# A list scheduler's cost table: one issue time for matmuls and transposes over the whole kernel

## The chip, the cores and the metric

The kernel runs on one core of a Trainium2 chip. The metric is the device time of one execution in microseconds; each kernel is run several times, and the median counts. One further execution is recorded by the profiler. The names of the profile are used throughout: PE is TensorE's matmuls, PEld its weight loads, DVE is VectorE, ACT is ScalarE, POOL is GpSimd, SP is the engine whose queue issues the weight transfers.

## The reference, cut to what matters

One layer of a bidirectional hybrid encoder with 512 tokens and 1024 channels in float32. Two branches mix tokens side by side, are gated and merged, and a SwiGLU feed-forward follows.

```python
h = rmsnorm(x, mix_norm[l])
p = h @ w_in[l]
rx, ry, qkv, z, ba, gates = jnp.split(p, SPLIT_IDX, axis=-1)
y_rnn = rglru_branch(rx, ry, ...) @ w_rnn_proj[l]
y_dn = deltanet_branch(qkv, z, ba, ...) @ w_dn_proj[l]
g_rnn, g_dn = jnp.split(jax.nn.sigmoid(gates), 2, axis=-1)
x = x + (g_rnn * y_rnn + g_dn * y_dn) @ w_out[l]
h = rmsnorm(x, ffn_norm[l])
gt, up = jnp.split(h @ w_gate_up[l], 2, axis=-1)
x = x + (jax.nn.silu(gt) * up) @ w_down[l]
...
return rmsnorm(x, final_norm)
```

The recurrent branch (RG-LRU) works on 1536 channels in 12 blocks of 128: a short convolution, two sigmoid gates per direction, an exponential, a square root, and a linear scan forwards and backwards. The DeltaNet branch has 8 heads of 128: convolutions and SiLU for q, k and v, norms, a triangular solve for each chunk of tokens, and a state that is carried from chunk to chunk, in both directions.

## The kernel before, in words

**Tiling.** Channels lie on the 128 partitions and the 512 tokens along the free axis. A weight matrix is streamed in pieces of 128 x 1024 floats (768 or 256 for the branch projections). Each piece is loaded into `wraw` by SP's queue, rounded to fp32r by ScalarE (`whi`), and the remainder is formed by VectorE (`wlo`). The activations are split the same way into `hh` and `hl`. A projection of one output block is then three sets of matmuls into one PSUM bank: `whi` with the high and with the low activations, and `wlo` with the high ones. With 8 contraction steps that is 24 matmuls of 512 columns. `whi` and `wlo` have two buffers each, `wraw` three.

**Stages.** The norm and its transposes come first (some 23 us). Then the recurrent blocks run in four groups of three (`rg_front`, `rg_mid`, `rg_out`); a group's sigmoids, its tanh and exponentials, its square roots and the GELU of its second projection need different tables on ScalarE, and each change of table is an `ACT_TABLE_LOAD`. Then the DeltaNet heads go through in four pairs (`dn_front`, `dn_mats`, `dn_inverse`, `dn_state`, `dn_out`), interleaved with the gate projections (`rnn_gate`, `dn_gate`). In `dn_inverse` a chain of some sixty small VectorE instructions inverts 32 x 32 blocks by substitution and ends in two stream transposes, after which TensorE joins the blocks. `dn_state` is a chain between TensorE, which fills a PSUM bank, and ScalarE or VectorE, which copies or combines it for the next step. At the end of the branch `dn_part(0, 6, n)` projects the first six heads and `dn_part(6, 2, n)` the last two, whose tiles come out of the last `dn_out`. The output projection, the feed-forward (gate/up products by a seven-product scheme) and the down projection follow.

**Order.** No instruction is issued where it is written. Every call on an engine goes through the class `Rec`, which books a cost in ns for it and appends it to `Plan.ops` with its dependences on tiles. At the end `Plan.order` runs a list schedule over all of them: it keeps a time for each engine, and lets an engine that is free in that plan take the ready instruction with the smallest due time whose buffers can be had. The due times come from the place in the source (`plan.t`, advanced by `spend`) and from a list of 156 numbers, `TIMES`, which give the base time of each stage in units of 100 ns. For ScalarE an instruction that needs another table than the loaded one is put back by `SWITCH` (12,000 ns) in that comparison, but taken when nothing else is ready. The engines then run the found sequence in program order, with semaphores for the dependences, so that a cost in the table changes nothing but the sequence.

**The table for TensorE.** `Rec` books a matmul by its columns n, lines 351 to 356:

```python
if op == "transpose" and self.plan.fixed > 3:
    cost = 110
elif four_:
    cost = 33 if cols == 32 else 81 if cols == 64 else n * 4 / 2.4
else:
    cost = max(n / 2.4, 107 if rhs.dtype == F32R else 54) + (self.plan.fixed if rhs.dtype == F32R else 2.5)
```

`four_` is true for plain float32 operands. `Plan.__init__` sets `fixed` to 2.5 (line 78), and the body of the kernel sets it to 13.3 at line 1209, behind the first half of the output projection. ScalarE and VectorE costs are booked 10% longer than their formulas (`SLACK`), and results pass between engines after fixed delays (`LAG`).

Of the kernel before, what the change touches and what calls it, by code (L numbers as in the profile page):

```python
# [54 lines left out]
class Plan:  # L55
# [10 lines left out]
    def __init__(self, nc):  # L66
        self.nc = nc
        self.ops = []
        self.where, self.bases = [], []
        self.t = self.base = 0.0  # L70
        self.stage = 0
        self.tags = {}
        self.tile_tag = {}
        self.hist = {}
        self.keep = set()
        self.extra = ()
        self.admit = ()
        self.fixed = 2.5

    def tile(self, pool, shape, dt, tag, bufs, name):  # L80
        ap = pool.tile(list(shape), dt, tag=tag, name=name, bufs=bufs)
# [298 lines left out]
def trunk(ctx: ExitStack, tc: tile.TileContext, x, mix_norm, w_in, rg_conv_w, rg_conv_b, rg_wa, rg_ba, rg_wx, rg_bx,  # L380
# [3 lines left out]
    plan = Plan(nc)  # L384
# [34 lines left out]
    def four(dt=F32, shape=(P, 2, 512)):  # L419
        return new(t4, shape, "t4", N4, dt)  # L420
# [747 lines left out]
    def weights_w(src):  # L1168
        now = plan.t
        raw = new(wp, (P, 2, 512), "wraw", 3)  # L1170
        hi = four(F32R)
        lo = four(F32R)
        plan.t = now - 20
        Q.dma_start(raw, src)
        plan.t = now - AHEAD
        A.copy(hi, raw)
        V.tensor_tensor(lo, raw, f(hi), ALU.subtract)
        plan.t = now
        return hi, lo
# [12 lines left out]
    def wo_part(k2, half):  # L1192
        return wo[:, 2 * k2:2 * k2 + 2, half * 512:(half + 1) * 512]
# [12 lines left out]
        V.tensor_scalar(sb, sa, 1.0 / D, EPS, ALU.mult, ALU.add)  # L1206
        ssh.append(sb)
    ws = [weights_w(wo_part(k2, 1)) for k2 in range(4)]
    plan.fixed = 13.3
    a1 = [four(shape=(P, 4, 256)) for _ in range(2)]  # L1210
    a2 = [four(shape=(P, 4, 256)) for _ in range(2)]
    for c in range(NT):
# [240 lines left out]
```

## Time and profile before

| | us |
|---|---|
| median of 3 runs | 1095.43 |
| their range | 1092.89 to 1096.24 |
| the profiled execution | 1094.72 |
| its span in the profile | 1093.0 |

| engine | busy, us | instructions |
|---|---|---|
| PE | 1069.0 | 6916 |
| DVE | 828.9 | 1489 |
| ACT | 625.3 | 1125 |
| POOL | 44.2 | 93 |

The profiled execution is one of its own, and its time and span differ by 1.7 us that lie outside the recorded instructions. All instructions carry line 374, the line of the recording helper, so that places are told by tile and time: `mm`, `ax` and `st` are the three kinds of PSUM bank, `t` is any of the shared work tiles. In a timeline a row is start, length, engine, line, operation, result and operands, the number of instructions merged, and in brackets the idle time before them with what ended it. A row's time may overlap the next row's, since instructions of one engine overlap in flight; the distance between two starts is the time that the engine spends on one.

### The profile page before, as it was taken

The numbers are of one execution on the slowest core, as the hardware profiler recorded it, in microseconds if no ns is written. First come the engines' busy times: TensorE is split into PE (matmuls) and PEld (weight loads), VectorE is DVE, ScalarE is ACT, GpSimd is POOL, SyncE is SP. The second block draws the span as 40 slices with busy tenths as digits, with TensorE's granted clock in tenths as the row PEclk, the third lists the DMA queues.
The fourth block names the chain that finished last, engine by engine and source line by source line (L and its number), as shares of the span: only waits on it lengthen the run. The fifth ranks groups of instructions, "written<-read, shape, count | busy, mean of one in ns | idle before, by whom it ended". The sixth has DMA issues, their size and how long they took to land.

```text
span 1093.0 us, 17606 instructions
## 1 busy us (share of the span) xinstructions
PE 1069.0 (98%) x6916; PEld 933.9 (85%) x6916; DVE 828.9 (76%) x1489; ACT 625.3 (57%) x1125; POOL 44.2 (4%) x93
## 2 busy tenths in 40 slices
PE   7999999999999999999999999999999999999997
PEld 6988788887888887888798887789999999988886
DVE  6777999779895898599749847768988988872432
ACT  6868987887348644765575254446544454451223
POOL 2000000002020100020010000000000000000000
PEclk9999999999999999999999999999999999999999
DMA  7333323232321133104302313442233333333222
GB/s 194 96 107 86 97 63 87 82 92 76 102 78 55 49 102 97 40 20 119 93 18 58 93 54 111 134 127 67 81 114 114 99 99 117 103 110 97 97 97 77
DMA packets 160787, 98.40 MB, mean 90 GB/s; under 512 B 4800, under 2 KB 151344, under 8 KB 160704
## 3 DMA queue, kind: packets, MB, share of 16 engines
q1 hardware_dynamic: 159232, 93.99, 29.5%
q10 hardware_dynamic: 1184, 3.15, 0.8%
q8 instruction: 54, 0.88, 0.3%
q0 software_dynamic: 288, 0.13, 0.1%
q14 instruction: 29, 0.24, 0.1%
HBM read 95.17 MB, written 2.10 MB: 89 GB/s over the span
## 4 chain that ended last, share of the span: by engine, by line
PE 83%; DVE 3%; ACT 2%; issue 0%; DVEq 0%; ACTq 0%
PE mm L374 48%; PE ax L374 20%; PE st L374 15%; DVE t L374 3%; ACT na L374 1%; ACT t L374 1%; DVE wlo L374 0%; ACT ax L374 0%; ACT whi L374 0%; ACT L374 0%; DVE na L374 0%; DVEq L1448 0%; ACT drt L374 0%; ACT rst L374 0%; DVE nq L374 0%
## 5 line engine op out<-in xcount | busy, mean ns | idle before, releaser
L374 ACT CAST whi<-wraw 128x1024 fp32r<-128x1024 f32 (+2 forms) x150 | 146.4, 977 | 220.2 <-PE mm L374 109.9
L374 DVE TENSOR_TENSOR wlo<-wraw,whi 128x1024 fp32r<-128x1024 f32 (+2 forms) x149 | 169.2, 1137 | 129.4 <-ACT whi L374 94.4
L374 PE MATMUL mm<-hh,whi 128*128 128x512 f32 (+2 forms) x704 | 242.0, 356 | 1.1 <-ACT whi L374 1.1
L374 PE MATMUL mm<-hl,whi 128*128 128x512 f32 (+2 forms) x704 | 241.6, 355 | 0.0
L374 DVE TENSOR_TENSOR t<-t,t 128x512 fp32r<-128x512 f32 (+17 forms) x414 | 213.2, 525 | 15.7 <-ACT t L374 8.6
L374 PE MATMUL mm<-hh,wlo 128*128 128x512 f32 (+1 forms) x688 | 153.9, 355 | 1.1 <-DVE wlo L374 1.1
L374 PEld LDWEIGHTS mm<-hh,whi 128*128 128x128 f32 (+1 forms) x704 | 132.4, 188 | 18.7 <-ACT whi L374 1.9
L374 PEld LDWEIGHTS mm<-hl,whi 128*128 128x128 f32 (+1 forms) x704 | 132.4, 188 | 17.1 <-DVE hl L374 0.2
L374 PEld LDWEIGHTS mm<-hh,wlo 128*128 128x128 f32 x688 | 116.0, 189 | 18.6 <-DVE wlo L374 1.5
L374 PE MATMUL ax<-t,t 32*32 32x32 f32 (+3 forms) x876 | 89.8, 262 | 0.8 <-issue 0.7
L374 PE MATMUL mm<-t,whi 128*128 128x512 f32 x320 | 82.0, 398 | 2.6 <-ACT t L374 1.8
L374 DVE SCALAR_TENSOR_TENSOR t<-mm,par,t 128x511 f32<-128x511 f32 (+1 forms) x108 | 80.0, 744 | 3.7 <-ACT t L374 2.9
L374 PEld LDWEIGHTS ax<-t,t 128*128 128x128 f32 (+1 forms) x876 | 74.7, 153 | 8.2 <-ACT t L374 1.6
L374 ACT ACT_TABLE_LOAD x58 | 74.4, 1283 | 5.8 <-PEq L1439 1.7
L374 ACT CAST t<-t 128x512 fp32r<-128x512 f32 (+1 forms) x95 | 64.5, 685 | 22.7 <-DVE t L374 21.0
L374 PEld LDWEIGHTS mm<-t,whi 128*128 128x128 f32 x320 | 59.9, 190 | 17.4 <-ACT t L374 2.4
L374 PE MATMUL mm<-t,t 128*128 128x256 f32 (+1 forms) x372 | 66.4, 322 | 0.0
L374 ACT ACTIVATE t<-t 128x128 f32<-128x128 f32 (+4 forms) x84 | 45.8, 558 | 23.8 <-DVE t L374 20.3
L374 PEld LDWEIGHTS mm<-t,t 128*128 128x128 f32 x372 | 54.7, 191 | 5.2 <-ACT t L374 0.3
L374 PE MATMUL mm<-t,wlo 128*128 128x512 f32 x160 | 43.0, 396 | 0.0
L374 PE MATMUL st<-hh,whi 128*128 128x512 f32 (+1 forms) x112 | 42.0, 378 | 0.0
L374 PE MATMUL st<-hl,whi 128*128 128x512 f32 (+1 forms) x112 | 41.8, 378 | 0.0
(219 smaller groups left out, 1804.9 us busy)
## 6 DMA issues: line engine op xcount, KB each, us to landing
wraw<-in_w_in_dram SPq DMA_DIRECT2D x72, 512.0 KB, 3.8
wraw<-in_w_gate_up_dram SPq DMA_DIRECT2D x44, 512.0 KB, 3.9
wraw<-in_w_down_dram SPq DMA_DIRECT2D x22, 512.0 KB, 3.7
wraw<-in_w_rnn_proj_dram SPq DMA_DIRECT2D x16, 384.0 KB, 3.6
wraw<-in_w_out_dram SPq DMA_DIRECT2D x8, 512.0 KB, 4.5
wraw<-in_w_dn_proj_dram SPq DMA_DIRECT2D x8, 384.0 KB, 3.6
t<-in_x_dram SPq DMA_DIRECT2D x4, 512.0 KB, 5.1
na<-in_x_dram ACTq DMA_DIRECT2D x4, 512.0 KB, 6.1
```

The costliest lines, as they stand in the source:

```text
L374: self.plan.add(e, lambda: real(*a, **kw), outs, ins, cost, tail, table)
```

## The change

The start value of `fixed` becomes 13.3, and the line that set it later is dropped. So all fp32r matmuls ahead of that line are booked 10.8 ns longer, and all transposes ahead of it (plain float32, 128 columns of result) at 110 ns in place of 512/2.4 = 213 ns. `TIMES`, `SLACK`, `LAG`, the dependences and the instructions stay as they are; the list schedule is run again with the new table.

```diff
         self.keep = set()
         self.extra = ()
         self.admit = ()
-        self.fixed = 2.5
+        self.fixed = 13.3
...
     ws = [weights_w(wo_part(k2, 1)) for k2 in range(4)]
-    plan.fixed = 13.3
     a1 = [four(shape=(P, 4, 256)) for _ in range(2)]
```

## The prediction

> **What bounds the kernel now.** I read the page first, then busy time by stage, then the timelines of the places where TensorE waits.
>
> ```profile
> span 1093.0 us, 17606 instructions
> PE 1069.0 (98%) x6916; PEld 933.9 (85%) x6916; DVE 828.9 (76%) x1489; ACT 625.3 (57%) x1125; POOL 44.2 (4%) x93
> 30.00:690.00 660.00, 649.47 (x4071) 543.93 (x4071) 528.52 (x984) 427.14 (x784) 37.58 (x72) 1.00 0.27 78
> 690.00:1093.00 403.00, 396.75 (x2709) 369.64 (x2707) 282.34 (x461) 178.58 (x303) 0.00 (x0) 1.00 0.33 102
> 60.00:93.00 33.00, 26.10 (x40) 1.00 0.34 96
> 93.00:145.00 52.00, 45.24 (x59) 1.00 0.29 82
> ```
>
> The third and fourth lines are stages: from, to, length, then busy time of PE, PEld, DVE, ACT and POOL. The last two give ACT alone. TensorE is the bound nearly everywhere. No instruction's work changes, so only its idle time can. From 30 to 690 us, where the two orders differ most, that is 660 - 649.5 = 10.5 us, plus a slow clock and small gaps between overlapping records. More than some 12 us can't be won; the loss has no such limit. Around 93 to 145 us ScalarE is nearly full too, with 52 - 45.24 = 6.76 us idle.
>
> **What the edit changes in the table.** It moves the 13.3 to the start. Until line 1209 a 512-column fp32r matmul was booked at 512/2.4 + 2.5 = 215.8 ns; now it is 226.6. A 128-column transpose falls from 213 to 110.
>
> ```profile
> 275.83 1.98 PE L374 MATMUL mm<-hh,wlo 128*128 128x512 f32 x8
> 277.65 0.39 PE L374 MATMUL mm<-hh,whi 128*128 128x512 f32 x1
> na<-in_x_dram ACTq DMA_DIRECT2D x4, 512.0 KB, 6.1
> ```
>
> Eight matmuls take 277.65 - 275.83 = 1.82 us, 227 ns each, so the new entry is the true one here. The program issues the same matmuls, casts and transfers; the two built orders differ in sequence, and ScalarE carries 60 table loads in place of 58. The last 571 rows of TensorE's order are the same. The weight queue on SP shifts only in its first 50 rows, mostly gate loads against main weights. None of TensorE's waits below is on a transfer, so I cost that at nothing; what hides it is that a landed tile waits for its cast, and if this cover went, the cast would start late by what the transfer lacks. The four transfers on ScalarE's queue (last line above, 6.1 us to land) move ahead of one 0.84 us cast near 667 us; their tile is first used after 690 us, behind the first half of the output projection, and that hides them.
>
> **Part A, the recurrent-gate stage: ScalarE's queue.**
>
> ```profile
> 104.12 1.28 ACT L374 ACT_TABLE_LOAD   x1
> 105.41 1.09 ACT L374 ACTIVATE t<-st 128x512 f32<-128x512 f32 x2
> 110.21 0.78 ACT L374 ACTIVATE t<-mm,zero_t,par 128x512 f32<-128x512 f32 x1 [3.70 <-PE mm L374]
> 110.89 1.98 ACT L374 CAST whi<-wraw 128x1024 fp32r<-128x1024 f32 x2
> 112.77 1.34 ACT L374 ACTIVATE t<-t,rgt 128x512 f32<-128x512 f32 x2
> 116.05 0.60 ACT L374 CAST t<-t 128x512 fp32r<-128x512 f32 x1
> 119.43 1.32 ACT L374 ACTIVATE t<-t,rgs 128x512 f32<-128x512 f32 x2
> L374 ACT CAST t<-graw 128x512 fp32r<-128x512 f32 x12 | 7.4, 616 | 1.1 <-DMA graw<-in_rg_wx_dram 1.1
> 111.97 0.50 PE L374 MATMUL mm<-hh,whi 128*128 128x512 f32 x1 [1.11 <-ACT whi L374]
> 115.73 0.39 PE L374 MATMUL mm<-hh,whi 128*128 128x512 f32 x1
> 120.63 2.12 PE L374 MATMUL mm<-hh,wlo 128*128 128x512 f32 x8 [1.12 <-DVE wlo L374]
> ```
>
> Before the cast at 110.89 the new order has four more table loads, 4 x 1.28 = 5.1 us, because it fits exponentials between the sigmoids of two blocks. It also issues those blocks' gate matmuls 4 to 5 us later on TensorE, so ScalarE would have stood idle there, and 3.70 us idle stand at 110.21. I take the loads as absorbed up to this cast. The row at 110.89 is two casts back to back. In the new order the second follows a gate cast (0.6, pipelined 0.55), two tanh (1.34), a load (1.28), two exponentials (1.32) and a cast (0.55): 5.0 us more, so it ends near 111.9 + 5.0 + 1.05 = 118.0. TensorE wants it at 115.73, at an unchanged place: 2.3 us late. The wait at 120.63 (start 1.3 us late) goes in exchange: VectorE's order there hardly changes, and its tile is ready when TensorE gets there. Net **+1.1 us**. Late next would be the cast at 120.66 for the block after, but there the new order gives TensorE more to do first.
>
> ```profile
> 144.28 1.05 ACT L374 CAST whi<-wraw 128x1024 fp32r<-128x1024 f32 x1
> 148.63 3.78 ACT L374 ACTIVATE t<-t,rgt 128x512 f32<-128x512 f32 x6
> 152.31 0.61 ACT L374 CAST t<-t 128x512 fp32r<-128x512 f32 x1
> 151.60 0.39 PE L374 MATMUL st<-hh,whi 128*128 128x512 f32 x1
> ```
>
> The cast at 144.28 is put behind the six tanh, another load (1.28) and an exponential (0.7): 152.3 + 2.0 + 1.05 less the 0.95 that it vacated, 154.4, against a use at 151.60 (0.2 later in the new order). That is 2.6 late; TensorE is already 1.1 behind, which leaves **+1.5**. Bounds for A: nothing, if ScalarE gives back its idle time ahead of the cast (33 - 26.10 = 6.9 and 6.76 us, against 15.3 us more work summed with the old durations); 15.3 less the old margin of 6.5 = 8.8, if none. I take +2.6, nearest to the walk along the rows.
>
> In sentences that the sum can do without: the Trainium skill, page "ScalarE: Activation LUTs", section "What ACT_TABLE_LOAD costs", charges each switch with about 1283 ns and a drain of about 1380 ns. The trace agrees with the load, but not here with the drain: 104.12 + 1.28 = 105.40, and the next activation starts at 105.41. By that page four loads would cost another estimated 5.5 us and the sum would be near 1102.
>
> **Part B, the ends of the DeltaNet substitutions.** Four times a VectorE chain of some 30 us hands its result to TensorE.
>
> ```profile
> 324.41 4.17 DVE L374 STREAM_TRANSPOSE t<-t 128x1024 f32<-128x1024 f32 x2
> 329.07 0.75 PE L374 MATMUL ax<-t,na 32*32 32x32 f32 x64
> 437.05 0.74 PE L374 MATMUL ax<-t,na 32*32 32x32 f32 x64 [1.09 <-DVE t L374]
> 534.72 0.47 PE L374 MATMUL ax<-t,na 32*32 32x32 f32 x33 [0.41 <-DVE t L374]
> 630.60 0.74 PE L374 MATMUL ax<-t,na 32*32 32x32 f32 x64 [0.75 <-DVE t L374]
> ```
>
> In the new order TensorE has 1.59, 1.36 and 4.53 us less work ahead of the first, third and fourth of these places, and 0.45 more ahead of the second (matmuls counted at 227 ns); VectorE has 0.96 less ahead of the fourth, and the same ahead of the others. The first had 329.07 - 328.58 = 0.49 us to spare: +1.1. The second gives 0.45 back, the third loses 1.36. At the fourth the chain no longer stands behind the low-part cast that follows it, and it can use idle time of VectorE: 0, though 3.4 if it can't. Sum **+2.0**; bounds 0 (idle time absorbs all) and +5.4.
>
> **Part C, the covers of the state chain.** After each short group TensorE fills the time until ScalarE's copy.
>
> ```profile
> 642.96 1.05 PE L374 MATMUL st<-t,na 128*128 128x128 f32 x8
> 643.77 0.94 PE L374 MATMUL mm<-t,wlo 128*128 128x512 f32 x3
> 645.23 1.05 PE L374 MATMUL st<-t,t 128*128 128x128 f32 x8
> 644.05 0.59 ACT L374 COPY t<-st 128x512 f32<-128x512 f32 x1 [0.21 <-PE st L374]
> ```
>
> From 643.77 to 645.23, 1.46 us of fill cover a copy that ends at 644.64. Of 59 such steps 31 had six matmuls (1.36 us) or more; in the new order 27 have, and 29 have about five (1.13 us) against 24. A free ScalarE needs about 0.9 us, so most stay covered; a copy behind a 1.05 us cast does not. I take **+0.4**, bounds -1 and +2.
>
> **Part D, the last two heads' transposes.**
>
> ```profile
> 676.66 1.03 PE L374 MATMUL ax<-ident,t 128*128 128x128 f32 x8
> 678.05 1.40 DVE L374 SCALAR_TENSOR_TENSOR t<-ax,par,t 128x512 f32<-128x512 f32 x2
> 678.83 1.28 ACT L374 CAST t<-t 128x512 fp32r<-128x512 f32 x2 [2.29 <-DVE t L374]
> 679.50 0.50 PE L374 MATMUL mm<-t,whi 128*128 128x512 f32 x1 [1.81 <-ACT t L374]
> 680.71 1.11 PE L374 MATMUL mm<-t,whi 128*128 128x512 f32 x3 [0.70 <-DVE t L374]
> 681.30:685.50 4.20, 4.20 (x12) 2.83 (x12) 2.41 (x5) 1.33 (x3) 0.00 (x0) 0.60 0.11 31
> ```
>
> Here TensorE has nothing to fill in: 1.81 + 0.70 us idle, and then a granted clock of 0.60 (the last line's third number from its end), in which twelve matmuls take 4.20 in place of 12 x 0.227 = 2.72 us. Together 4.0. The new order puts these transposes 7.5 us earlier and ten matmuls of the previous projection behind them (2.3 us), then the rest in between. The low part still comes about 0.6 us late and VectorE's normalised tile perhaps 0.4. I take **-3.0**, bounds -4.2 and -1. Beside this: the Trainium skill, page "TensorE: Matmul & The Clock Gate", section "What's actually happening", halves the clock after an idle window of about 3.4 us. The trace agrees with the half clock, but not with the length: the two waits here, 2.5 us in all, were enough. By the page the clock's 1.5 us would not be there to win, and the sum would be near 1098.
>
> **Sum.** 2.6 + 2.0 + 0.4 - 3.0 = +2.0 us. The profiled execution took 1094.72 us, 1.7 beside its span; that makes **1096.7 us**. That execution lies 0.7 under the median of the runs shown, 1095.43, so the forecast is 0.1% over the median.
>
> **Rivals.** *ScalarE becomes the bound of the gate stage* (slower): its idle time there stays a wait for TensorE, as at 110.21, and all 8.8 us of A reach the casts: 1094.7 + 8.8 + 2.0 + 0.4 - 3.0 = **1102.9**. For it: 87% busy. Against: the later gate matmuls leave room. It decides once over half of the 13.7 us idle can't be given back. *A truer table packs better* (faster): A and B are absorbed, C gives 1 and D 4.2: **1089.5**. For it: 227 ns, and the idle rows of B and D; against it: the unchanged priorities, under which the casts above move back. *The edit changes nothing that counts*: the stalls only trade places, **1094.7**; for it TensorE's equal work, against it the concrete rows of D.
>
> **How the numbers follow.** The forecast has 0.39 (its own range 1093 to 1100), ScalarE's queue 0.29, better packing 0.21, nothing 0.11. The bounds sum to 1094.7 + 0 + 0 - 1 - 4.2 = 1089.5 and 1094.7 + 8.8 + 5.4 + 2 - 1 = 1109.9; both ends together are unlikely, so the range is **1089 to 1107**. About 0.3% (3.3 us) is what a measurement of this kernel can tell from no change. Over 1098.7 lie the second case and a third of the first: 0.43. Under 1092.1 lies the third and a little of the first: 0.23. The rest, 0.34, is within.
>
> **What would show it.** Right: a wait of TensorE for the cast near 116 and one near 154 us; the waits of 1.81 and 0.70 us near 680 and the clock of 0.60 gone; waits for VectorE of 1 to 2 us at the four substitution ends; 60 table loads. Wrong: ScalarE waiting for TensorE at 110 for less than a microsecond while TensorE waits for it (then A is larger), or TensorE idle for some 4 us at the fourth substitution end, where B has 0.

## The result, and the profile after

The changed kernel takes 1097.75 us (median of 11 runs, 1096.56 to 1101.12) against 1094.81 for the kernel before beside it. The ratio of the means is 1.0032 (of these medians 1.0027), 95% interval 1.0022 to 1.0042. It is slower, by about the 0.3% that a measurement of this kernel can tell. The profiled execution took 1096.93 us, 2.2 more than that of before.

The head of the page, then the table of stretches (from, to, length, busy time of PE, PEld, DVE, ACT and POOL, granted clock, DMA share, GB/s):

```profile
span 1095.2 us, 17616 instructions
PE 1070.3 (98%) x6916; PEld 933.7 (85%) x6916; DVE 826.6 (75%) x1489; ACT 626.6 (57%) x1127; POOL 46.1 (4%) x93
```

```profile
30.00:690.00 660.00, 648.65 (x4060) 541.55 (x4059) 524.01 (x979) 425.59 (x782) 39.46 (x72) 1.00 0.27 77
...
93.00:145.00 52.00, 48.36 (x203) 38.75 (x202) 46.46 (x52) 46.29 (x61) 1.43 (x3) 0.97 0.25 70
118.00:123.50 5.50, 5.28 (x16) 4.27 (x17) 5.50 (x8) 4.88 (x9) 0.00 (x0) 0.69 0.07 15
```

Work and counts are the same but for ScalarE's two more table loads; the other eight new instructions are semaphore operations. TensorE has lost time, and the third and the fourth line show one place: a clock of 0.69, with VectorE busy for all of the 5.50 us.

To see where the 2.2 us lie I took, for each matmul of both traces, its start less the usual distances (227 ns for 512 columns, 120 for 256, 112 for a transpose, 52 and 15 for the small tiles) of everything ahead of it on TensorE. What remains is time lost up to there, and the difference of the two kernels at the same amount of work done says where one lost more:

| stretch, in us of TensorE's work | after less before, us | the forecast's term |
|---|---|---|
| up to 100 (113 us of the trace) | -0.2 | 0 |
| 100 to 200 (113 to 214 us of the trace): the gate stage | +4.8 | A: +2.6 |
| 200 to 300 | -1.3 | 0 |
| 300 to 640: the DeltaNet heads | +3.3 | B and C: +2.4 |
| 640 (668 us of the trace) to the end: the last two heads' transposes | -4.4 | D: -3.0 |
| sum | +2.2 | +2.0 |

The places in the timeline of the changed kernel (start, length, engine, operation; idle time ahead in brackets). TensorE in the gate stage:

```profile
115.31 0.39 PE L374 MATMUL mm<-hl,whi 128*128 128x512 f32 x1
118.22 0.79 PE L374 MATMUL mm<-hh,whi 128*128 128x512 f32 x1 [2.52 <-ACT whi L374]
118.81 0.63 PE L374 MATMUL mm<-hl,whi 128*128 128x512 f32 x1
119.24 0.63 PE L374 MATMUL mm<-hh,whi 128*128 128x512 f32 x1
```

ScalarE, whose cast at 117.13 is the one waited for:

```profile
102.31 2.01 ACT L374 ACTIVATE t<-t 128x1024 f32<-128x1024 f32 x2
...
110.65 1.03 ACT L374 CAST whi<-wraw 128x1024 fp32r<-128x1024 f32 x1
...
114.76 1.34 ACT L374 ACTIVATE t<-t,rgs 128x512 f32<-128x512 f32 x2
116.60 0.62 ACT L374 CAST t<-t 128x512 fp32r<-128x512 f32 x1 [0.50 <-DVE t L374]
117.13 1.04 ACT L374 CAST whi<-wraw 128x1024 fp32r<-128x1024 f32 x1
```

The square roots at 102.31 began in the kernel before at

```profile
101.14 2.96 ACT L374 ACTIVATE t<-t 128x1024 f32<-128x1024 f32 x3
```

TensorE stood still for 118.22 - 115.31 - 0.23 = 2.68 us and then ran at half speed: the next eight matmuls took 121.71 - 118.22 = 3.49 us (121.71 is the start of the ninth) in place of 8 x 0.227 = 1.82, six of them 0.43 us from one to the next. That is another 1.7 us. The cast stands behind two exponentials and a small cast that itself waited for VectorE, whose chain began 1.17 us later with the square roots. TensorE at the ends of the four substitutions and at the last transposes:

```profile
331.44 0.75 PE L374 MATMUL ax<-t,na 32*32 32x32 f32 x64 [0.57 <-DVE t L374]
...
443.14 0.74 PE L374 MATMUL ax<-t,na 32*32 32x32 f32 x64 [0.42 <-DVE t L374]
...
539.09 0.75 PE L374 MATMUL ax<-t,na 32*32 32x32 f32 x64 [0.81 <-DVE t L374]
...
631.64 0.74 PE L374 MATMUL ax<-t,na 32*32 32x32 f32 x64 [0.83 <-DVE t L374]
...
675.77 0.60 PE L374 MATMUL ax<-ident,t 128*128 128x128 f32 x4
676.12 0.48 PE L374 MATMUL mm<-t,whi 128*128 128x512 f32 x1
676.44 0.60 PE L374 MATMUL ax<-ident,t 128*128 128x128 f32 x4
676.79 2.10 PE L374 MATMUL mm<-t,whi 128*128 128x512 f32 x8
...
687.11 0.73 PE L374 MATMUL mm<-t,wlo 128*128 128x512 f32 x2 [0.51 <-DVE wlo L374]
```

All four ends wait now, each for less than a microsecond. Behind the transposes TensorE goes straight on with earlier matmuls; of the 4 us that stood there, 0.5 of waiting is left.

### The profile page after: what moved, and what is told of

It is laid out like the page before. It is cut to its first block, busy times and chain, and to the rows that moved or that the text cites. A ratio compares the mean times of both kernels' runs of the same rounds, so it can differ in the third digit from the quotient of the medians.

```text
span 1095.2 us, 17616 instructions
## 1 busy us (share of the span) xinstructions
PE 1070.3 (98%) x6916; PEld 933.7 (85%) x6916; DVE 826.6 (75%) x1489; ACT 626.6 (57%) x1127; POOL 46.1 (4%) x93
## 4 chain that ended last, share of the span: by engine, by line
PE 87%; DVE 7%; ACT 4%; issue 1%; DMA 1%; SPq 0%; DVEq 0%
PE mm L374 50%; PE ax L374 22%; PE st L374 15%; DVE t L374 5%; ACT t L374 2%; DVE wlo L374 1%; ACT na L374 1%; DMA wraw<-in_w_in_dram 1%; DVE na L374 1%; ACT whi L374 1%; ACT L374 0%; DVE hl L374 0%; ACT ax L374 0%; SPq L374 0%; ACT hh L374 0%
## 5 line engine op out<-in xcount | busy, mean ns | idle before, releaser
L374 DVE TENSOR_TENSOR t<-t,t 128x512 fp32r<-128x512 f32 (+16 forms) x414 | 212.4, 524 | 17.0 <-ACT t L374 10.4
```

The lines of the kernel that those rows point to most:

```text
L374: self.plan.add(e, lambda: real(*a, **kw), outs, ins, cost, tail, table)
```

## Experiments

All runs in one table. "Loss" is the measure above against the trace of before, by stretch of TensorE's work; the medians stand beside 1093.9 to 1094.8 us for the kernel before in the same runs. The stretch up to 100, -1.4 to +0.8, is left out.

| run | median, us | ratio (95%) | 100-200 | 200-300 | 300-640 | 640-end |
|---|---|---|---|---|---|---|
| the change | 1097.75 | 1.0032 (1.0022-1.0042) | +4.8 | -1.3 | +3.3 | -4.4 |
| matmuls only | 1104.90 | 1.0104 (1.0091-1.0118) | +4.9 | -0.1 | +8.7 | -2.9 |
| transposes only | 1124.73 | 1.0279 (1.0265-1.0293) | 0.0 | -0.5 | +26.0 | +4.6 |
| from the DeltaNet heads on | 1102.24 | 1.0071 (1.0058-1.0084) | 0.0 | -1.2 | +6.9 | -0.1 |
| last pair of heads only | 1093.24 | 0.9991 (0.9982-0.9999) | 0.0 | 0.0 | 0.0 | -1.3 |
| 12.3 for 13.3 | 1108.84 | 1.0133 (1.0118-1.0148) | +15.6 | -1.6 | +3.2 | -3.5 |
| before, cast back | 1099.29 | 1.0047 (1.0035-1.0060) | +4.5 | 0.0 | -0.6 | +0.8 |
| after, cast forward | 1099.60 | 1.0049 (1.0035-1.0062) | +5.7 | -1.2 | +4.0 | -4.1 |
| after, four moved | 1100.22 | 1.0059 (1.0046-1.0073) | +6.0 | -1.2 | +3.1 | -3.8 |
| before, three moved | 1093.05 | 0.9993 (0.9984-1.0002) | -0.7 | 0.0 | -0.6 | -0.3 |
| after, exponentials together | 1099.97 | 1.0049 (1.0033-1.0066) | +7.2 | -1.3 | +3.0 | -3.6 |
| searched, from after | 1114.03 | 1.0186 (1.0172-1.0200) | +6.6 | +0.1 | +16.7 | -4.8 |
| searched, from last pair only | 1111.73 | 1.0158 (1.0144-1.0172) | +7.5 | +0.8 | +14.2 | -3.7 |

Where rows run one and the same sequence (the changed kernel and its three edits, or the kernel before and its two, all behind 200) they differ by up to 1.1 us in a stretch. A difference of a microsecond between two rows is therefore not told from none.

### What the late cast costs

In the kernel before, the cast is put seven ScalarE operations later in the found sequence (with `moved`, the operations that need it); no other engine's order changes.

```diff
         todo = plan.order()
+        acts = [i for i in todo if plan.ops[i][0] == "ACT"]
+        end = todo.index(acts[acts.index(cast) + 7]) + 1
...
+        todo = [i for i in todo[:end] if i not in moved] + moved + todo[end:]
```

> The kernel before with one instruction elsewhere: the same cast stands seven ScalarE operations later (two tanh, a table load, two exponentials, a tanh and two small casts come first), so that it ends near 118.5 us against a use at 115.73. Theory of the late cast: a wait of 2.8 us, some 1.6 us of half clock behind it, less the 1.3 us wait for the low part at 120.63 that goes: +3.1 us, about 1097.9; +1.8, about 1096.6, if the wait of 1.31 us at 249 gives that much back. Theory that the half clock belongs to something else in the changed order: +1.5 or less, no granted clock under 0.9 near 120.

TensorE's timeline, and the stretch behind it:

```profile
115.31 0.39 PE L374 MATMUL mm<-hl,whi 128*128 128x512 f32 x1
119.70 0.50 PE L374 MATMUL mm<-hh,whi 128*128 128x512 f32 x1 [4.00 <-ACT whi L374]
```

```profile
119.00:124.00 5.00, 4.30 (x12) 3.39 (x13) 3.79 (x5) 4.06 (x6) 0.00 (x0) 0.66 0.42 111
```

One cast, late by 4.2 us, costs 4.5 us that nothing behind it gives back: 4.2 of waiting, some 1.7 of slow clock, less the 1.3 us wait for the low part that goes. (The expected 3.1 was for a wait of 2.8.) The wait at 249 us stayed as it was, so its going in the changed kernel belongs to the new sequence there.

A late cast thus brings a wait and half clock, as in the change. It does not explain the whole of the change's +4.8, because the wait is shorter there: 2.68 of waiting and 1.7 of slow clock, less 1.4 for the low part (the 1.28 and a slow matmul behind it), make 3.0 us at that place. The other 1.8 lie in four smaller stalls of 0.4 to 0.6 us near 141, 155, 181 and 200 us, which no run moved alone.

### Whether moving the cast takes it away

```diff
         todo = plan.order()
+        todo.remove(cast[1])
+        todo.insert(todo.index(cast[0]) + 1, cast[1])
```

> The changed kernel with one instruction elsewhere: ScalarE's cast that TensorE waits 2.68 us for at 118.22 stands directly behind the cast before it, five operations earlier. Theory of the late cast: the wait of 2.68 us and the slow clock behind it (1.7 us) go, the wait of 1.3 us for the low part near 120 comes back, and the time falls by about 3.1 us to some 1094.7. Theory that ScalarE's whole work bounds the stage: the operations that the cast passes come 1.05 us later, TensorE waits for one of them instead, and the time stays at 1097 to 1098.

It doesn't. (In the sequence the cast passes six operations and a table load; the text above says five.) TensorE, and VectorE's row for what it then waits for, in this run and in the kernel before:

```profile
118.67 0.39 PE L374 MATMUL mm<-hl,whi 128*128 128x512 f32 x1
122.47 2.58 PE L374 MATMUL mm<-hh,wlo 128*128 128x512 f32 x8 [3.41 <-DVE wlo L374]
124.85 0.63 PE L374 MATMUL mm<-hh,whi 128*128 128x512 f32 x1
```

```profile
121.20 2.36 DVE L374 TENSOR_TENSOR wlo<-wraw,whi 128x1024 fp32r<-128x1024 f32 x2
```

```profile
119.36 1.22 DVE L374 TENSOR_TENSOR wlo<-wraw,whi 128x1024 fp32r<-128x1024 f32 x1
```

The first of the two low parts ends some 1.2 us after 121.20, and TensorE starts at 122.47. Behind the late cast stood an equally late low part, covered only because TensorE was already waiting. The 3.6 us from 118.67 + 0.23 to 122.47 add up: 1.28 were waited there in the kernel before, the low part starts 1.84 us later, and TensorE is through with the matmuls ahead of it 0.46 us earlier (118.90 for 119.13 + 0.23), having four fewer of them.

So the next edit, with a helper that puts one operation ahead of another in the found sequence, moves four operations: the late cast (756); both low parts (865 and 757), ahead of two scans and three small operations; and the next cast (980) by five operations, ahead of a small cast that waits for VectorE:

```diff
+        put(756, 1592)
+        put(865, 443)
+        put(757, 443)
+        put(980, 729)
```

> The changed kernel with four instructions elsewhere near 110 to 125 us: the late cast directly behind the one before it, the next cast four operations earlier, and two low parts on VectorE ahead of the two scans that they stood behind. The run before had the late cast moved alone, and TensorE waited 3.58 us for a low part in its place. Theory of two chains equally late (cast on ScalarE, low part on VectorE): with both moved neither wait remains, the 2.68 us and the 1.7 us of slow clock go, and the time falls by some 4.3 us to 1093.4. Theory that the whole stage is bound by ScalarE's or VectorE's work: TensorE waits 2 to 4 us for a third thing before 160 us, and the time is 1096 to 1098.

```profile
128.49 0.44 PE L374 MATMUL mm<-hh,whi 128*128 128x512 f32 x1
132.59 1.22 PE L374 MATMUL ax<-t,t 128*128 128x512 f32 x2 [3.66 <-ACT t L374]
```

Both waits are gone, and 3.9 us appear ten microseconds later, at the gate matmuls of a block whose split activations come through VectorE and ScalarE. VectorE is full here, so the low parts moved forward push its two scans back, from 116.48 to 119.04 us, and what hangs on the scans is late instead. The theory of two late chains falls; that of a stage bound by the work behind the square roots fits, though the expected 1096 to 1098 was too low. The last three of these moves in the kernel before:

> The kernel before with the same two low parts and the same next cast moved forward. Theory of two chains: the wait of 1.28 us at 120.63 goes and nothing takes its place, 1093.1 us against 1094.4. Theory that the stage is bound by the work: the wait of 1.3 us reappears before 160 us, and the time stays at 1094.4.

There the wait of 1.3 us becomes one of 0.6 near 132, a gain of 0.7 us that the timing (0.9993, 0.9984 to 1.0002) doesn't tell from none. So neither kernel gains by these moves.

### Whether the table loads are the cause

Two exponentials that stand alone between two table loads each are put with the next ones.

```diff
         todo = plan.order()
+        for i in (418, 419):
+            todo.remove(i)
+            todo.insert(todo.index(422), i)
```

> The changed kernel with two exponentials of the first block, which each stand alone between two table loads near 82 and 90 us, put right ahead of the next exponential at 97.5: 56 table loads in place of 60, 4 x 1.28 = 5.1 us less work on ScalarE ahead of the square roots. Theory that the loads were absorbed by ScalarE's idle time (the prediction's step): the square roots at 102.31 don't come earlier, since they wait for what TensorE delivers, the wait of 2.7 us at 118 stays, and the time stays within 1 us of the changed kernel's 1097.7. Theory that the loads fill ScalarE's queue up: the square roots and with them VectorE's low parts come 2 to 4 us earlier and the time falls by 2 to 4 us.

ScalarE's groups and its timeline:

```profile
L374 ACT ACT_TABLE_LOAD x56 | 71.8, 1283 | 5.7 <-PEq L1441 1.7 <-PE ax L374 1.5 <-PE mm L374 0.8
```

```profile
85.89 0.69 ACT L374 ACTIVATE t<-ax,par 128x512 f32<-128x512 f32 x1 [2.69 <-PE ax L374]
...
94.05 0.69 ACT L374 ACTIVATE t<-ax,par 128x512 f32<-128x512 f32 x1 [2.24 <-PE ax L374]
...
103.70 2.01 ACT L374 ACTIVATE t<-t 128x1024 f32<-128x1024 f32 x2
```

Four loads fewer, and ScalarE idles instead, waiting for TensorE's gate matmuls: the loads were absorbed, as the prediction had it. But the two exponentials now stand in the part that isn't idle, the square roots begin 1.4 us later, TensorE's wait for the cast grows from 2.68 to 3.95 us, and the time from 1097.75 to 1099.97, which neither theory had. The square roots' start passes on nearly one for one (1.39 us there, 1.27 at the wait): from there to the cast runs a chain through a full VectorE. In the change that chain starts 1.17 us late, and not because of these four loads; that it is the gate matmuls, which the new sequence issues later, is what these idle times suggest, but no run moved them alone.

### Whether the change is the sum of its parts

The matmuls' entry alone, and the transposes' entry alone, each from the start:

```diff
+        self.turns = False
...
-                if op == "transpose" and self.plan.fixed > 3:
+                if op == "transpose" and self.plan.turns:
...
+    plan.turns = True
```

> One part of the change alone: the matmuls at 226.6 ns from the start, the transposes still at 213 ns up to line 1209. Theory of places: the gate stage has hardly a transpose, so its loss of 3.5 to 4.8 us comes back in full, the DeltaNet heads lose some 3, and the last two heads' transposes stay uncovered: about 1102. Theory of shuffling: the sequence of the gate stage differs from both kernels' and its waits too; anything from 1092 to 1104, with no wait near 118 us in common with the changed kernel.

```diff
-        self.fixed = 13.3
+        self.fixed = 2.5
...
-                if op == "transpose" and self.plan.fixed > 3:
+                if op == "transpose":
...
+    plan.fixed = 13.3
```

> The other part alone: transposes at 110 ns from the start, matmuls at 215.8 ns up to line 1209. Theory of places: the gate stage as before, the transposes near 680 us covered: 1094.4 - 4.4 = 1090.0, with up to 2 us more or less from the DeltaNet heads. Theory of shuffling: the ends of the substitutions have waits unlike either kernel's, and the time is anywhere from 1091 to 1099.

The matmuls alone bring the changed kernel's loss in the gate stage back in full, as the theory of places had it and shuffling hadn't: +4.9, with TensorE's wait at the same place:

```profile
118.18 0.50 PE L375 MATMUL mm<-hh,whi 128*128 128x512 f32 x1 [2.55 <-ACT whi L375]
```

The transposes alone leave the gate stage as it was. So far the change is its parts. In the heads it isn't: +8.7 and +26.0 us for the halves, +3.3 for both. Neither theory had these times: 1104.90 against 1102 and 1092 to 1104, and 1124.73 against 1090 and 1091 to 1099. With the transposes alone the stretch of the third pair's state chain reads

```profile
585.00:629.00 44.00, 28.77 (x167) 23.60 (x166) 30.77 (x94) 13.55 (x40) 0.00 (x0) 0.81 0.05 12
```

and its longest wait is this one:

```profile
619.85 1.97 PE L374 MATMUL ax<-ident,t 128*128 128x128 f32 x8 [7.63 <-DVE t L374]
```

44.00 - 28.77 = 15.2 us of it are idle, at a clock of 0.81. Up to 622 us TensorE has only the heads' own small matmuls and transposes there; the projections that fill the stretch in the other kernels stand elsewhere in this sequence. Two more kernels switch the new entries on later, from the first DeltaNet line and from the last pair of heads (a line `plan.fixed = 13.3` at each place, 2.5 before it):

> The old table up to the first line of the DeltaNet heads, the new one from there on. Theory of places (the change is the sum of what happens at single places: +3.5 us in the recurrent-gate stage, +3.3 in the DeltaNet heads, -4.4 at the last two heads' transposes): the gate stage is as before, with no wait for the cast near 118 us and 58 or 59 table loads, the transposes near 680 are covered, and the time is that of before + 3.3 - 4.4 = -1.1, about 1093.7 us. Theory of shuffling (any new sequence loses or wins some 3 us anywhere, and the table's truth has nothing to do with it): the waits in the DeltaNet heads fall at other places than in the changed kernel, the last transposes may or may not be covered, and the time is anywhere from 1091 to 1098.

> The kernel before with the new table for the last pair of DeltaNet heads alone. Theory of places: everything up to some 560 us is as before, the waits of 1.97 and 0.98 us and the slow clock near 680 go, and the time falls by 4.4 us to some 1090.4. Theory of shuffling: the sequence before the transposes changes as well, new waits of 1 to 3 us appear between 560 and 675 us, and the time is 1093 to 1096.

The same entries over the heads, started from another state of the plan, cost +6.9 in place of +3.3 and win 0.1 in place of 4.4 at the last transposes. From the last pair on they cover the transposes with the previous projection, but the low part is late instead:

```profile
PE mm L374 <- DVE wlo L374: 3.0, 3, 1.4
```

(the table of waits: in all, times, longest; 1.9 us of it in the transposes' projection, the rest at 120), and the net is -1.3, little more than the 1.1 by which rows of one sequence differ. The theory of places missed by 8.5 and 2.8 us. Shuffling fares little better: 1102.24 is 4.2 over its range, and 1093.24 lies within it, but without the new waits between 560 and 675 us that it rested on (0.0 in that stretch). What the runs show is that the same entries have another price in the heads when the plan comes to them in another state; how much another, neither theory told.

### Whether the truth of the entry decides

```diff
-        self.fixed = 13.3
+        self.fixed = 12.3
```

> The changed kernel with 12.3 in place of 13.3: the table's matmul 1 ns (0.4%) shorter. Theory that the truth of the entry decides: the sequence is as good as the changed kernel's, 1097 to 1099. Theory of shuffling: any other entry gives another sequence with its own waits, several us away. An estimate, from a replay of the found sequence with each instruction's duration and the delays between engines as the traces of the two kernels show them (it comes out 7 to 9 us short of the measured span for the six sequences run so far), puts this one 9.5 us over the changed kernel, about 1106.

One nanosecond per matmul makes 11 us:

```profile
148.98 1.65 PE L374 MATMUL ax<-t,t 128*128 128x512 f32 x3 [2.95 <-ACT t L374]
152.89 1.65 PE L374 MATMUL ax<-t,t 128*128 128x512 f32 x3 [2.26 <-ACT t L374]
...
176.13 0.50 PE L374 MATMUL mm<-hh,whi 128*128 128x512 f32 x1 [2.84 <-ACT whi L374]
```

The gate stage loses 15.6 us here, and the estimate by replay was nearer (1106) than the theory of truth. So how true the entry is doesn't set the time by itself; what counts is the sequence that falls out. What truth does bring is seen in the list schedule's own clock. These are its reckoning and no times of the chip:

```
list schedule's own clock, us          entry 2.5   entry 13.3
the late cast of the gate stage ends     106.65      117.07
TensorE is free for its first matmul     109.39      114.64
that matmul starts                       109.39      117.39
the whole schedule ends                 1064.2      1082.7
```

With the new entry it reckons a wait of 2.74 us at that matmul; the chip shows 2.68. It foresees the wait and takes it, since it picks by due time what is ready and never looks back for a sequence without the wait.

### Whether a better sequence can be had from the traces

A search moves single instructions and short groups in the stored sequence and replays each candidate with durations and delays taken from the two traces; the kernel issues the result.

```diff
-        todo = plan.order()
+        todo = SEQUENCE
```

> The same instructions in a stored sequence: the changed kernel's own sequence, improved by a search that moves one instruction or a few earlier or later and keeps a move where the replay (durations and delays between engines as the traces of the two kernels show them) comes out no longer. Theory that the sequence at single places is what counts, and that the entry only chose among sequences: the estimate is 12 to 15 us under the replay of the changed kernel, so 1083 to 1088 us, with the waits at 118, 331, 443, 539 and 631 us gone or under 0.5 us. Theory that the stages are bound by the work of ScalarE and VectorE, or that the replay only fits its own errors: 1094 or more.

> The same search from another start, the sequence of the kernel with the new table for the last pair of heads alone (measured 1093.2). The estimate is 11 to 14 us under that one's replay: 1080 to 1084 us if sequences decide; 1092 or more if the replay only fits its own errors. The gate stage has the early sequence of the kernel before here, so that both starts ending at the same time would say that the early sequence is no limit either.

Both miss by 25 us or more, on the wrong side, and lie where the other theory had them (1094 or more, 1092 or more). In the gate stage TensorE still waits for the low part, and loses 6.6 and 7.5 us. In the sequence searched from after this wait stands at 121.95 us:

```profile
PE mm L727 <- DVE wlo L727: 3.1, 1, 3.1
```

Of the wait at this place the replay had left under 0.5 us. Behind the gate stage the waits are few, but the search split the groups of small tiles (the searched sequence from after, then the row that follows the undivided group at 329.07 in the kernel before):

```profile
333.79 0.24 PE L727 MATMUL ax<-t,na 32*32 32x32 f32 x2 [0.23 <-DVE t L727]
333.97 0.50 PE L727 MATMUL mm<-hh,whi 128*128 128x512 f32 x1
334.40 0.24 PE L727 MATMUL ax<-t,na 32*32 32x32 f32 x2
334.57 0.50 PE L727 MATMUL mm<-hl,whi 128*128 128x512 f32 x1
335.00 0.24 PE L727 MATMUL ax<-t,na 32*32 32x32 f32 x2
```

```profile
329.75 0.50 PE L374 MATMUL mm<-hh,whi 128*128 128x512 f32 x1
```

Undivided, 64 small matmuls take 329.75 - 329.07 = 0.68 us. Here two of them and one wide one take 0.60 in place of 0.02 + 0.23: each further piece costs about 0.35 us. It isn't the slow clock, which is 1.00 from 333 to 336 us, and not the change between plain float32 and fp32r either: four whole transposes and one wide matmul in the changed kernel take 676.44 - 675.77 = 0.67 us, no more than 4 x 0.112 + 0.227. The searched sequence has 44 stretches of 32 x 32 tiles and 27 of 64 x 64 in place of 9 and 10. The time beyond the usual distances at the matmuls that go into and out of such tiles is 21.4 us against 7.5, waits included, which is 13.9 of the 19.3 us that the span is longer. The replay had no price for such a change, and the search spent what looked free. So no sequence here beats both kernels clearly; the best are at 0.999 of before.

## Why the prediction came out as it did

The forecast was 1096.7 us; the median is 1097.75, the profiled execution 1096.93. That the sum is so near, +2.0 against +2.2, is partly luck: A came out 2.2 us and B with C 0.9 over their terms, and 1.3 us that no term named and 1.4 us in D came back.

- **Part A: the place was right, the size was not** (+2.6 against +4.8). The cast wanted at 115.73 was forecast 2.3 us late, with the wait for the low part going in exchange: measured 2.68 and 1.28, so +1.4 for +1.1. Not counted was the half clock behind such a wait, about 1.7 us, although the same text had read it off the waits near 680. The second cast was forecast at +1.5 and stalls TensorE by 0.44 at 155.47. Three more stalls of some 0.4 us, near 141, 181 and 200, weren't in the sum, and neither was the -1.3 at 249 us.
- **Loads absorbed: right.** Taking four away won nothing; ScalarE idled in their place.
- **"VectorE's order there hardly changes, and its tile is ready when TensorE gets there": true, but only because TensorE was late.** The cast moved alone shows the tile ready at 122.4, 3.6 us after TensorE could have used it. The prediction priced one instruction; what was late was the chain behind the square roots.
- **The rival of a bound gate stage (1102.9): half right.** Two edits moved the wait from the cast to the low part and then to the gate matmuls, and the loss didn't fall (5.7 and 6.0 us for 4.8) with the same sequence on TensorE. But what was full was VectorE behind the square roots, not ScalarE, which the rival named: ScalarE still idled 2.31 us at 110, and the 8.8 us were too much.
- **Parts B and C: +2.4 against +3.3.** The four ends wait 0.7, 0.6, 1.0 and 1.0 us in the stalls of the trace, where 1 to 2 us each were named as the sign. The first was forecast at +1.1 and shows +0.7, with another 0.55 at the next group, at 333.95; the fourth was forecast unchanged and is (0.9 before). With the groups that follow, the stretches at the four ends lost +1.2, -1.0, +0.7 and +0.6 us, +1.5 in all against +2.0. The larger part lies where no term looked: +1.8 between the first end and the second, with waits for VectorE of 0.94 us at 377.54 and 0.44 at 394.99. The rest of the heads comes to -0.1, so that C's +0.4 can't be told from nothing.
- **Part D: -3.0 against -4.4.** The forecast left a microsecond of lateness for the low part and the normalised tile; 0.7 us showed, once, and no slow clock.
- **"A truer table packs better" (1089.5) fell**: the truer entry lost, and 1 ns beside it costs 11 us more, so that its truth doesn't set the time by itself.

What held up was working from the two built sequences, place by place. Reasoning about the table in general would have told little: its halves alone cost 11 and 31 us.

## What to carry to other kernels

A cost table behind a greedy list schedule is a seed: an edit that makes it truer makes the schedule's own clock truer (here 1082.7 for 1095.2 us, where it was 1064.2 for 1093.0) and draws another sequence, whose value must be read from the sequence. Try the neighbours of such an entry too, because they show how wide the lottery is. The due times (`TIMES`) stayed as they were in every run here; whether the true entries would win with due times of their own was not tried. When one wait is moved by hand and returns at the next operand, stop moving and look for the start of the chain.

## What was not expected of the hardware

One wait of 2.52 us was enough for half speed over the next matmuls (0.43 us each, clock 0.69 in the stretch), as were 4.00 us before a stretch at 0.66. The price hardly depends on the length: in the seven traces with one such wait in the gate stage, 2.7 to 4.2 us long from the usual distance, the slow matmuls behind it lost 1.6 to 1.7 us; in an eighth, with the exponentials together, 2.8. The waits of 1.1 us near 112 and 120 in the kernel before left 0.23 us from matmul to matmul. The Trainium skill, page "TensorE: Matmul & The Clock Gate", section "What's actually happening", gives an idle window of about 3.4 us; here less did it.

Going from 128 x 128 tiles to 32 x 32 ones on TensorE and back cost about 0.35 us for each piece that a group was cut into, which is as much as 1.5 matmuls of 512 columns. In kernels with such tiles the groups are to be kept whole.
